# Two tiles' gate columns per branch-B unit, projected one unit later in a streaming encoder layer

## The chip, the cores and the metric

The kernel runs on one core of one Trainium2 chip. The metric is the device time of one execution in microseconds. The kernel before takes 2224.91 us, the median of three runs (2220.69 to 2227.12). The engines go by their names in the profile: PE is TensorE, DVE is VectorE, ACT is ScalarE, POOL is GpSimd, SP is SyncE (here it only issues DMAs).

## The reference

One layer over a prompt of 2048 rows and over 8 running sequences of 16 rows (one more tile of 128 rows), width 1024. Two mixers work side by side on the same normed input `h`: branch A, a differential softmax attention with 4 heads of two 64-wide parts, and branch B, a stick-breaking attention with 8 heads of 64.

```python
h, gate = adaln_modulate(x, c, norm_g, w_ada, b_ada)
qa, ka, va, za, qb, kb, vb, zb, ga, gb = split(h @ w_in)   # 4 x 512, 4 x 512, 2 x 1024 columns
# branch A: p = softmax of two score sets, w = p1 - lam * p2, oa = w @ va
# branch B: z = qb @ kb.T / 8
log_1m = where(kpos < qpos, log_sigmoid(-z), 0)
log_a  = log_sigmoid(z) + reverse_cumsum(log_1m) - log_1m
ob     = where(kpos < qpos, exp(log_a), 0) @ vb
ya = (rms_norm(oa) * silu(za)) @ w_branch_a
yb = (ob * silu(zb)) @ w_branch_b
y  = (sigmoid(ga) * ya + sigmoid(gb) * yb) @ w_out
x  = x + gate * y
```

The 2048 columns `ga` and `gb` of `h @ w_in` are the gate columns that this change moves. Nothing needs them before the last stage, which merges the branches.

## The kernel before, in words

**Units and tiles.** The projections and the prompt's attention are cut into 8 units, `u` = 0 to 7. Unit `u` is one pair of heads, `h = u // 2`, of branch A (`kind` 0, even `u`) or branch B (`kind` 1, odd `u`). In each unit 17 tiles of 128 rows are worked: first the sample rows (`t = NT = 16`), then the prompt's tiles 0 to 15. So there are 136 steps `(u, t)`.

**Projection.** For a step, `project` multiplies the tile's `h`, kept as two f16 halves, with the unit's 512 columns of `w_in`, also two halves: 24 matmuls of 128x512 at L467 into a bank `ps_mm`, in 12 pieces of two. ACT, DVE and, in branch A, POOL then make queries, keys and values of them. `h` of a tile comes from DRAM (`fetch_h`, 512 KB) into one of three buffers `hs`, taken in turn; a load into a buffer must wait for the last matmul that reads what lies there.

**Gates.** A unit of branch B also owns 512 gate columns: `GATES[u]` has width 512 for odd and 0 for even `u`. So a step of branch B has 24 more matmuls at L543 (`gate_piece`) into the one bank `ps_t`, an ACT evacuation at L548 into the one buffer `gt`, and a store of 256 KB at L551 into `g_d[t]`. The same bank `ps_t` serves the transposes of queries and keys (L561, L565) and small column sums (L235). A step of branch A has no gates. Only the last five tiles of unit 7 (`late`) have theirs put off to the end, with pieces of their own.

**Scores.** `scores` works one tile of queries against all keys up to it, in chunks of 512 keys: two matmuls (L708, L709) into one of three banks `ps_s`, and a masking one (L712) on the diagonal. There are `2 * (t // 4 + 1)` chunks for tile `t`, so 80 in a unit. In branch B each chunk gets two sigmoids on ACT (L134), a running product on DVE (L682), a multiplication on POOL (L688), then the f16 halves on ACT (L616) and DVE (L619), a transposing DMA (L626, `wt<-sc_n`), and the product with the values on PE (L769, L770). In branch A there is a maximum on DVE (L602), the exponentials on ACT, the same transposing DMA, and L765 to L767 on PE. Tiles with high `t` are long, those with low `t` short.

**What sets the order.** The projections' pieces stand in one `line`; the loop at the end takes as many of them per scoring step as an estimate of that step's length says (`position`, `take`), about five steps ahead of the scores (`LEAD`). So while unit 1's last tiles are scored, unit 2's first tiles are projected. The pieces of scoring, projecting and preparing weights are interleaved by cost. The framework's scheduler then orders each engine's instructions and may move one behind others where its operands come later.

**Weight buffers.** 16 buffers of 4 KB per partition (`wa`, `wb`) go round in the list `free`. A unit's cut weights take four (`bufs[0:4]`), its gate weights four more (`bufs[4:8]`); `begin` gives them back when the next unit's first step starts. `prepare_unit` takes buffers for the unit after, and so do the key and norm passes (`norms`).

Of the kernel before, what the change touches and what calls it, by code (L numbers as in the profile page):

```python
# [21 lines left out]
AF = mybir.ActivationFunctionType  # L22
# [6 lines left out]
KT = D // P  # L29
# [4 lines left out]
NT = SEQ // P  # L34
# [28 lines left out]
LATE_ORDER = (NT - 3, NT - 1, NT - 2, NT - 5, NT - 4)  # L63
LATE_SHARE = (0, 20, 20, 20)
LEAD = 5.0
TILE_TIME = 0.6
SAMPLE_TIME = 0.3

GATES = [(u // 2 * 512, u % 2 * 512) for u in range(8)]
# [55 lines left out]
def layer_kernel(ctx: ExitStack, tc: tile.TileContext, a: dict):  # L125
    nc = tc.nc
    V, S, G, T = nc.vector, nc.scalar, nc.gpsimd, nc.tensor
    load = nc.sync.dma_start
# [11 lines left out]
    def kept(x):  # L140
        tc.keep_in_program_order(x)
        return x
# [45 lines left out]
    g_d = [dram.tile([P, 2 * D], F32, name=f"g_d{t}") for t in range(NT + 1)]  # L188
# [14 lines left out]
    free = buffers_of_4k("wa", 8)  # L203
# [7 lines left out]
    def bank(tag, dt=F32):  # L211
        return ps.tile([P, 512 if dt == F32 else 1024], dt, tag=tag, name=f"ps_{tag}", bufs=BANKS[tag])
# [120 lines left out]
    units = [None] * 8  # L333
# [68 lines left out]
    def finish_unit(u):  # L402

        U = units[u]
        sw, sh = U["sw"], sh_box[0]
        sc = con.tile([P, 7], F32, name=f"usc{u}")

        V.tensor_tensor(out=sc[:, 0:1], in0=U["fsq"], in1=nh2, op=ALU.mult)
        sq = scales(sc[:, 0:1], con, f"sq{u}")

        V.tensor_tensor(out=sc[:, 1:2], in0=sw[:, 1:2], in1=sh[:, 1:2], op=ALU.mult)
        V.tensor_tensor(out=sc[:, 2:3], in0=sc[:, 1:2], in1=sq[:, 0:1], op=ALU.mult)

        V.tensor_scalar(out=sc[:, 3:4], in0=sq[:, 1:2], scalar1=sq[:, 1:2], scalar2=0.125, op0=ALU.mult, op1=ALU.mult)
        V.tensor_scalar(out=sc[:, 4:5], in0=sc[:, 3:4], scalar1=-1.0, scalar2=None, op0=ALU.mult)

        if U["kind"] == 0:
            V.tensor_tensor(out=sc[:, 5:6], in0=sq[:, 1:2], in1=ls[:, 1:2], op=ALU.mult)
        else:
            V.tensor_scalar(out=sc[:, 5:6], in0=sq[:, 1:2], scalar1=2.0 ** -STICK, scalar2=None, op0=ALU.mult)  # L420
        if "sg" in U:

            V.tensor_tensor(out=sc[:, 6:7], in0=U["sg"][:, 1:2], in1=sh[:, 1:2], op=ALU.mult)
        U["sc"], U["sq"], U["k"], U["v"] = sc, sq, {}, {}
# [13 lines left out]
    def late(u, t):  # L438
        return u == 7 and NT - LATE <= t < NT

    def fetch_h(u, t):
        ahead[u, t] = hs[len(fetched) % 3].bitcast(F16).rearrange("p (f k n) -> p f k n", f=2, n=P)
        fetched.append(t)
        load(out=ahead[u, t], in_=hT_d[t // 4][:, t % 4, :, :, :])

    def project(U, t):

        kind, h, sc, sq = U["kind"], U["h"], U["sc"], U["sq"]
        g, i = t // 4, t % 4
        box = {}  # L450
# [18 lines left out]
        def piece(n):  # L469
            if n == 0:  # L470
                start()
            for j in range(2 * n, 2 * n + 2):
                mm(j)
            if n == 11:
                finish()
# [54 lines left out]
                load(out=s_d[U["u"]][:, 6:8, :], in_=vt.rearrange("p c f d -> p c (f d)"))  # L530
            U["q16", t], U["k16", t] = qb, k16

        g0, gw = GATES[U["u"]]
        per = 1024 // gw if gw else 0

        def gate_piece(n):

            if n == 0:
                box["g"] = bank("t")
            for j in range(per * n, per * n + per):  # L540
                hi, wi = ((0, 0), (0, 1), (1, 0))[j % 3]
                k = j // 3
                x = T.matmul(box["g"][:, 0:gw], box["h"][:, hi, k, :], U["wg"][k // per][:, k % per, wi, :], start=(j == 0), stop=(j == 3 * KT - 1))  # L543
                if late(U["u"], t) and j == per * n:
                    kept(x)
            if per * n + per == 3 * KT:
                gt = gts[:, 0:512]
                x = S.activation(out=gt[:, 0:gw], in_=box["g"][:, 0:gw], func=AF.Identity, scale=sc[:, 6:7])  # L548
                if late(U["u"], t):
                    kept(x)  # L550
                load(out=g_d[t][:, g0 : g0 + gw], in_=gt[:, 0:gw])  # L551

        U["gates", t] = box, [lambda n=n: gate_piece(n) for n in range(3 * KT // per if gw else 0)]
        return [lambda n=n: piece(n) for n in range(12)] + ([] if late(U["u"], t) else U.pop(("gates", t))[1])

    def transpose_qk(U, t):
        g, i = t // 4, t % 4
# [424 lines left out]
    def begin(u, t):  # L982
        if t == NT:
            if u > 0:
                free.extend(units[u - 1]["bufs"])
            finish_unit(u)

    def projection(m):
        u, t = steps[m]
        made = []  # L990

        def piece(i):
            if i == 0:
                begin(u, t)
                made.extend(project(units[u], t))
            if i == H_AT and not at_hand and m + 1 < len(steps) and steps[m + 1] not in ahead:
                fetch_h(*steps[m + 1])
            made[i]()

        return [lambda i=i: piece(i) for i in range(12 + (0 if late(u, t) else 3 * GATES[u][1] // 128))]  # L1000

    def late_gates(t):

# [418 lines left out]
    for n in range(len(steps) + 2):  # L1422
        made, qk, side = [], [], []
        if n < len(steps):
            u, t = steps[n]
# [215 lines left out]
```

## Time and profile before

| | |
|---|---|
| median of three runs | 2224.91 us (2220.69 to 2227.12) |
| the profiled execution, its own time | 2226.87 us |
| its span, first to last instruction | 2225.0 us |
| PE busy | 2048.1 us, 92% of the span |
| DVE / ACT / POOL busy | 1743.2 / 1605.3 / 719.5 us |
| mean granted PE clock | 0.98 |
| projection matmuls, L467 | 3120, busy 391.7 + 380.1 us |
| gate matmuls, L543 | 1632 (68 tiles of 24), busy 243.6 + 151.3 us |

Times are microseconds from the start of the span unless marked ns. A matmul's mean ns is its own length from start to end; matmuls overlap, so 24 in a row take much less than 24 of these. In the groups of instructions, what stands after the second bar is the idle time of the engine just before them, and what ended it. Windows cut the span into stretches and give each engine's busy time in them, the granted PE clock (PEclk) and the share of the DMA engines.

### The profile page before, as it was taken

What the parts mean: (1) busy time and instruction counts of PE and PEld (TensorE: products, weight loads), DVE (VectorE), ACT (ScalarE), POOL (GpSimd) and SP (SyncE); (2) the same over time, 40 slices, a digit from 0 to 9 for tenths busy, and PEclk for the clock granted to TensorE, in tenths of its full rate; (3) what the DMA queues carried; (4) which work ended last, traced back from release to release, by engine and by line L of the source; (5) the groups of instructions that cost most, each with busy time, mean ns of one, the idle gap of its engine ahead of it and who ended that gap; (6) DMA issues with size and microseconds to landing.
All of it is one profiled execution on the core that took longest, in us unless ns stands there. A gap on an engine that the chain in (4) does not pass through costs nothing.

```text
span 2225.0 us, 41210 instructions
## 1 busy us (share of the span) xinstructions
PE 2048.1 (92%) x14472; PEld 1089.3 (49%) x14472; DVE 1743.2 (78%) x3787; ACT 1605.3 (72%) x3212; POOL 719.5 (32%) x620
## 2 busy tenths in 40 slices
PE   3999999999999999999989998999997789899997
PEld 1545555555555455555554544555454344444443
DVE  5668868889886788988678888887689778787864
ACT  3978677788877787978777788876588575666531
POOL 0523024366311444742034365301345312211210
PEclk9999999999999999999999999999999899999999
DMA  9777669799796889979888999876677999889752
GB/s 333 261 246 183 128 151 224 181 221 209 184 266 164 217 199 207 212 192 227 190 207 203 182 237 223 231 171 136 151 165 174 192 280 251 217 250 235 188 155 67
DMA packets 824977, 451.03 MB, mean 203 GB/s; under 512 B 556122, under 2 KB 763274, under 8 KB 824256
## 3 DMA queue, kind: packets, MB, share of 16 engines
q1 hardware_dynamic: 823820, 448.01, 82.6%
q8 instruction: 113, 1.85, 0.4%
q14 instruction: 96, 0.79, 0.1%
q10 hardware_dynamic: 948, 0.39, 0.1%
HBM read 229.87 MB, written 86.02 MB: 142 GB/s over the span
## 4 chain that ended last, share of the span: by engine, by line
PE 27%; DVE 8%; DMA 7%; ACT 5%; issue 3%; POOL 2%; SPq 1%; DVEq 0%; POOLq 0%; ACTq 0%
PE ps_mm L467 7%; PE ps_t L543 6%; PE ps_o L1540 5%; PE ps_mm L1506 3%; DMA wt<-sc_n 2%; PE ps_s L708 1%; DVE sc_n L682 1%; PE ps_s L709 1%; DMA hs<-hT_d 1%; DMA hs<-o_d 1%; DMA dwt<-dsc 1%; ACT sc_p L134 1%; POOL sc_p L688 1%; PE ps_o L769 1%; ACT ps_s L134 1%
## 5 line engine op out<-in xcount | busy, mean ns | idle before, releaser
L688 POOL TENSOR_TENSOR sc_p<-sc_p,sc_n 128x127 f32<-128x127 f32 (+7 forms) x192 | 312.2, 1629 | 665.5 <-DVE sc_n L682 516.0
L467 PEld LDWEIGHTS <-hs 128*128 128x128 f16 x3120 | 293.3, 99 | 326.3 <-DMA hs<-hT_d 11.6
L467 PE MATMUL ps_mm<-wa,hs 128*128 128x512 f16 x1590 | 391.7, 382 | 10.8 <-DMA hs<-hT_d 9.2
L467 PE MATMUL ps_mm<-wb,hs 128*128 128x512 f16 x1530 | 380.1, 382 | 0.0
L682 DVE TENSOR_TENSOR_SCAN sc_n<-ps_s,sc_n,zero_t 128x512 f32<-128x512 f32 x192 | 245.4, 1278 | 30.6 <-ACT ps_s L134 25.1
L543 PE MATMUL ps_t<-wa,hs 128*128 128x512 f16 x1020 | 243.6, 381 | 3.3 <-DVE qst L576 2.3
L543 PEld LDWEIGHTS <-hs 128*128 128x128 f16 x1632 | 154.9, 98 | 186.2 <-DVE qst L576 6.3
L708 PE MATMUL ps_s<-k,qst 128*128 128x512 f16 (+3 forms) x640 | 222.8, 349 | 24.1 <-DVE sc_n L682 20.7
L619 DVE TENSOR_TENSOR sc_n<-sc_p,sc_n 128x128 f16<-128x128 f32 (+7 forms) x192 | 213.6, 1115 | 37.3 <-ACT sc_n L616 36.7
L134 ACT ACTIVATE sc_p<-ps_s,usc 128x512 f32<-128x512 f32 (+3 forms) x320 | 204.7, 640 | 36.0 <-PE ps_s L709 24.3
L709 PE MATMUL ps_s<-k,qst 128*128 128x512 f16 (+3 forms) x640 | 223.1, 349 | 0.0
L616 ACT CAST sc_n<-sc_p 128x128 f16<-128x128 f32 (+7 forms) x192 | 155.6, 811 | 60.6 <-POOL sc_p L688 59.9
L134 ACT ACTIVATE ps_s<-ps_s,usc 128x512 f32<-128x512 f32 (+3 forms) x320 | 197.0, 616 | 0.0
L543 PE MATMUL ps_t<-wb,hs 128*128 128x512 f16 x612 | 151.3, 382 | 7.8 <-DMA hs<-hT_d 4.4
L769 PE MATMUL ps_o<-v,wt 128*128 128x128 f16 x1088 | 134.4, 223 | 25.5 <-DMA wt<-sc_n 25.5
L1540 PE MATMUL ps_o<-wo,wb 128*128 128x512 f16 x624 | 144.8, 388 | 1.7 <-ACT wb L1314 1.7
L602 DVE TENSOR_SCALAR_CACHE_REDUCE sc_p<-ps_s,usc 128x512 f32<-128x512 f32 (+3 forms) x160 | 106.2, 664 | 33.3 <-PE ps_s L709 22.0
L1549 POOL TENSOR_TENSOR x<-m,x 128x512 f32<-128x512 f32 x32 | 47.0, 1468 | 255.4 <-DVE m L1544 161.8
L769 PEld LDWEIGHTS <-wt 128*128 128x128 f16 x1088 | 100.4, 100 | 54.3 <-DMA wt<-sc_n 29.6
L770 PE MATMUL ps_o<-v,wt 128*128 128x64 f16 x1088 | 126.2, 195 | 0.0
L682 DVE TENSOR_TENSOR_SCAN sc_n<-ps_s,zero_t 128x128 f32<-128x128 f32 (+3 forms) x128 | 104.1, 814 | 26.2 <-ACT ps_s L134 26.2
L1506 PEld LDWEIGHTS <-wa 128*128 128x128 f16 x816 | 77.8, 98 | 92.7 <-issue 6.3
(380 smaller groups left out, 4538.5 us busy)
## 6 DMA issues: line engine op xcount, KB each, us to landing
hs<-hT_d SPq DMA_DIRECT2D x132, 512.0 KB, 4.7
g_d<-gt SPq DMA_DIRECT2D x68, 256.0 KB, 4.7
out_dram<-pr SPq DMA_DIRECT2D x204, 64.0 KB, 3.3
o_d<-o SPq DMA_DIRECT2D x136, 64.0 KB, 2.3
wa<-g_d SPq DMA_DIRECT2D x17, 512.0 KB, 4.2
wb<-g_d SPq DMA_DIRECT2D x17, 512.0 KB
hs<-o_d SPq DMA_DIRECT2D x17, 512.0 KB, 4.0
wide<-in_w_ada_dram SPq DMA_DIRECT2D x8, 1024.0 KB, 12.6
```

The costliest lines, as they stand in the source:

```text
L134: i = S.activation(**kw)
L467: T.matmul(box["p"], box["h"][:, hi, k, :], U["w"][k][:, wi, :], start=(n == 0), stop=(n == 3 * KT - 1))
L543: x = T.matmul(box["g"][:, 0:gw], box["h"][:, hi, k, :], U["wg"][k // per][:, k % per, wi, :], start=(j == 0), stop=(j == 3 * KT - 1))
L616: x = S.copy(out=hi, in_=src)
L619: V.tensor_tensor(out=lo, in0=src, in1=hi, op=ALU.subtract)
L682: V.tensor_tensor_scan(out=dst[:, lo : lo + n][:, ::-1], data0=src[:, 0:n][:, ::-1], data1=zero_t[:, 0:1].to_broadcast([P, n]), initial=fi ...
L688: G.tensor_tensor(out=p[:, 0:m], in0=p[:, 0:m], in1=n[:, 1 : m + 1], op=ALU.mult)
L708: T.matmul(p[:, 0:n], qst[:, c, :], kk[:, c, 0:n], start=True, stop=False)
L709: T.matmul(p[:, 0:n], qst[:, 2 + c, :], kk[:, c, 0:n], start=False, stop=not diag)
L769: T.matmul(po[:, c * P : (c + 1) * P], wt[:, wj, :], vt[:, c, :, :], start=first, stop=False)
L1506: T.matmul(pb, st["u"][:, ui * 8 + br * 4 + k, :], wb[br * 4 + k // 2 * 2 + j][:, wi, k % 2, :], start=(n == 0), stop=(n == 11))
L1540: T.matmul(po, st["y"][:, yi * 8 + k, :], wo[j * 4 + k // 2][:, wi, k % 2, :], start=(n == 0), stop=(n == 3 * KT - 1))
```

## The change

A new table `LATER = 1, 3` names two tiles. In the units 1, 3 and 5 the gate matmuls of the tiles 1 and 3 are left out of branch B's step, and put into the step of the same tile in the next unit, 2, 4 or 6 of branch A, behind that step's own 24 matmuls. They use the earlier unit's gate weights (`units[u - 1]`) and scale, and the `h` that branch A's step has loaded anyway. So these steps of branch A have 24 pieces, and those of branch B 12. Six tiles with 144 matmuls, six evacuations and six stores are moved in all; no instruction is added or removed. Unit 7's gates stay where they were. The gate weights' four buffers are given back five steps later: `begin` frees the first four at the next unit's first step, as before, and the other four when its tile 4 is begun.

```diff
+LATER = 1, 3
...
+    def gated(u, t):
+
+        if t in LATER and u < 7:
+            return u - 1 if u % 2 == 0 and u > 0 else None
+        return u if u % 2 == 1 and not late(u, t) else None
...
-        U["gates", t] = box, [lambda n=n: gate_piece(n) for n in range(3 * KT // per if gw else 0)]
-        return [lambda n=n: piece(n) for n in range(12)] + ([] if late(U["u"], t) else U.pop(("gates", t))[1])
+        made = [lambda n=n: piece(n) for n in range(12)]
+        if late(U["u"], t):
+            U["gates", t] = box, gate_pieces(U)
+        elif gated(U["u"], t) is not None:
+            made += gate_pieces(units[gated(U["u"], t)])
+        return made
...
         if t == NT:
             if u > 0:
-                free.extend(units[u - 1]["bufs"])
+                free.extend(units[u - 1]["bufs"][0:4])
             finish_unit(u)
+        if u > 0 and u % 2 == 0 and t == max(x for x in LATER if x < NT) + 1:
+            free.extend(units[u - 1]["bufs"][4:])
...
-        return [lambda i=i: piece(i) for i in range(12 + (0 if late(u, t) else 3 * GATES[u][1] // 128))]
+        return [lambda i=i: piece(i) for i in range(12 if gated(u, t) is None else 24)]
```

`gate_pieces(W)` is the old body of `gate_piece` with the unit `W` that owns the gate columns in place of `U`. Lines of the changed kernel have other numbers: L474 there is L467 before, L552 is L543, L576 and L580 are L561 and L565, L723, L724 and L727 are L708, L709 and L712, L784 and L785 are L769 and L770.

The first place is PE's order where branch A's tile 2 of unit 2 has just been projected: the first score chunk of tile 15, the last and longest of unit 1 (`ps_s<-k,qst`). Before, between products with the values and the transposes of the next tile:

```order
L769 LDWEIGHTS wt
L769 MATMUL ps_o<-v,wt 128x128
L708 LDWEIGHTS qst
L708 MATMUL ps_s<-k,qst 128x512
L709 LDWEIGHTS qst
L709 MATMUL ps_s<-k,qst 128x512
L712 LDWEIGHTS idb
L712 MATMUL ps_s<-masks,idb 128x128
L561 LDWEIGHTS k_6211
L561 MATMUL ps_t<-id_192,k_6211 128x128
```

Now, at the same score chunk, with `hs_180` the `h` of tile 1:

```order
L474 MATMUL ps_mm<-wa_172,hs_182 128x512
L784 LDWEIGHTS wt
L784 MATMUL ps_o<-v,wt 128x128
L723 LDWEIGHTS qst
L723 MATMUL ps_s<-k,qst 128x512
L724 LDWEIGHTS qst
L724 MATMUL ps_s<-k,qst 128x512
L727 LDWEIGHTS idb
L727 MATMUL ps_s<-masks,idb 128x128
L785 LDWEIGHTS wt
L785 MATMUL ps_o<-v,wt 128x64
L552 LDWEIGHTS hs_180
```

All 24 gate matmuls of tile 1 follow there in one piece; the scheduler has put them behind tile 2's columns and six matmuls of tile 3's (`hs_182`), not straight behind tile 1's.

The second place is PE's order where unit 2's own scores begin (tile 0, chunks of 128 keys). Before, this chunk stood among products with unit 1's values, and 14 matmuls into tile 5's projection:

```order
L467 LDWEIGHTS hs_181
L467 MATMUL ps_mm<-wb_1428,hs_181 128x512
L769 LDWEIGHTS wt
L769 MATMUL ps_o<-v,wt 128x128
L770 LDWEIGHTS wt
L770 MATMUL ps_o<-v,wt 128x64
```

Now the last gate matmuls of tile 3 (`hs_182`) stand ahead of it, and the projection is 19 matmuls into tile 4:

```order
L552 LDWEIGHTS hs_182
L552 MATMUL ps_t<-wa_173,hs_182 128x512
L723 LDWEIGHTS qst
L723 MATMUL ps_s<-k,qst 128x128
L724 LDWEIGHTS qst
L724 MATMUL ps_s<-k,qst 128x128
L727 LDWEIGHTS idb
L727 MATMUL ps_s<-masks,idb 128x64
L723 LDWEIGHTS qst
L723 MATMUL ps_s<-k,qst 128x128
```

So at this point 48 gate matmuls more, and 19 of the projection fewer, have been done since tile 14 of unit 1 than before.

The third place is PE's order where branch B gives the gates up, at a diagonal chunk of unit 2's tile 14 (384 keys), while unit 3's tile 2 is projected. Before, tile 1's gates stood ahead of it:

```order
L543 LDWEIGHTS hs_182
L543 MATMUL ps_t<-wb_1424,hs_182 128x512
L708 LDWEIGHTS qst
L708 MATMUL ps_s<-k,qst 128x384
L709 LDWEIGHTS qst
L709 MATMUL ps_s<-k,qst 128x384
L712 LDWEIGHTS idb
L712 MATMUL ps_s<-masks,idb 128x64
L467 LDWEIGHTS hs_180
L467 MATMUL ps_mm<-wa_170,hs_180 128x512
```

Now the transposes of a finished tile stand ahead of it:

```order
L580 LDWEIGHTS qbuf_214
L580 MATMUL ps_t<-id_192,qbuf_214 128x128
L723 LDWEIGHTS qst
L723 MATMUL ps_s<-k,qst 128x384
L724 LDWEIGHTS qst
L724 MATMUL ps_s<-k,qst 128x384
L727 LDWEIGHTS idb
L727 MATMUL ps_s<-masks,idb 128x64
L474 LDWEIGHTS hs_180
L474 MATMUL ps_mm<-wa_175,hs_180 128x512
```

By unit 3's first scores 48 gate matmuls are gone from the row.

More of the change, by code (lines that the diff above doesn't have):

```diff
@@ L531, in finish @@
             U["q16", t], U["k16", t] = qb, k16
[L533 to L551, printed above, removed]
@@ L553, in project, with gate_pieces, gate_piece @@
-        U["gates", t] = box, [lambda n=n: gate_piece(n) for n in range(3 * KT // per if gw else 0)]
-        return [lambda n=n: piece(n) for n in range(12)] + ([] if late(U["u"], t) else U.pop(("gates", t))[1])
+        def gate_pieces(W):
+            g0, gw = GATES[W["u"]]
+            per = 1024 // gw
+            def gate_piece(n):
+                if n == 0:
+                    box["g"] = bank("t")
+                for j in range(per * n, per * n + per):
+                    hi, wi = ((0, 0), (0, 1), (1, 0))[j % 3]
+                    k = j // 3
+                    x = T.matmul(box["g"][:, 0:gw], box["h"][:, hi, k, :], W["wg"][k // per][:, k % per, wi, :], start=(j == 0), stop=(j == 3 * KT - 1))
+                    if late(W["u"], t) and j == per * n:
+                        kept(x)
+                if per * n + per == 3 * KT:
+                    gt = gts[:, 0:512]
+                    x = S.activation(out=gt[:, 0:gw], in_=box["g"][:, 0:gw], func=AF.Identity, scale=W["sc"][:, 6:7])
+                    if late(W["u"], t):
+                        kept(x)
+                    load(out=g_d[t][:, g0 : g0 + gw], in_=gt[:, 0:gw])
+            return [lambda n=n: gate_piece(n) for n in range(3 * KT // per)]
```

## The prediction, made before the changed kernel ran

> **What bounds the kernel now.** I read the page's busy times first, then the chain that ended last, then the waits stage by stage.
>
> ```profile
> PE 2048.1 (92%) x14472; PEld 1089.3 (49%) x14472; DVE 1743.2 (78%) x3787; ACT 1605.3 (72%) x3212; POOL 719.5 (32%) x620
> PE 27%; DVE 8%; DMA 7%; ACT 5%; issue 3%; POOL 2%; SPq 1%; DVEq 0%; POOLq 0%; ACTq 0%
> PE ps_mm L467 7%; PE ps_t L543 6%; PE ps_o L1540 5%; PE ps_mm L1506 3%; DMA wt<-sc_n 2%; PE ps_s L708 1%; DVE sc_n L682 1%; PE ps_s L709 1%; DMA hs<-hT_d 1%; DMA hs<-o_d 1%; DMA dwt<-dsc 1%; ACT sc_p L134 1%; POOL sc_p L688 1%; PE ps_o L769 1%; ACT ps_s L134 1%
> ```
>
> PE leads with 92%, and the gate matmuls (L543) hold 6% of the span on the chain, second only to the projection. The change takes no matmul away; it can win only idle time of PE. So the question is where PE idles, and whether the moved matmuls land there. To cut the span by stages I count score matmuls in their order:
>
> ```profile
> L708 PE MATMUL ps_s<-k,qst 128*128 128x512 f16 (+3 forms) x640 | 222.8, 349 | 24.1 <-DVE sc_n L682 20.7
> ```
>
> 640 are 80 in each unit, 2 x (t // 4 + 1) for tile t, so the first of each tile is known. The windows below run from one such start to another. First three: from tile 12 of units 0, 2 and 4 (branch A) to the first scores of units 1, 3 and 5; there the B tiles 1 and 3 are projected now. Then three for each A unit 2, 4, 6: from tile 14 of the B unit before to the A unit's tile 0, from there to tile 4, and to tile 9.
>
> ```profile
> core 0: us, PE busy (x) PEld busy (x) DVE busy (x) ACT busy (x) POOL busy (x), PEclk, DMA share, GB/s
> 222.00:294.00 72.00, 69.13 (x486) 37.79 (x486) 52.75 (x136) 46.17 (x95) 0.00 (x0) 1.00 0.61 127
> 629.00:699.00 70.00, 67.50 (x469) 37.01 (x468) 49.60 (x135) 48.86 (x103) 2.24 (x2) 1.00 0.85 204
> 1041.00:1111.00 70.00, 69.37 (x470) 37.77 (x468) 49.27 (x133) 47.99 (x101) 2.24 (x2) 0.98 0.88 205
> 482.00:524.00 42.00, 38.48 (x310) 21.40 (x310) 40.55 (x49) 40.89 (x81) 31.82 (x24) 1.00 0.98 207
> 524.00:554.00 30.00, 27.24 (x222) 15.63 (x220) 28.01 (x70) 23.10 (x55) 18.12 (x19) 0.94 0.91 206
> 554.00:594.00 40.00, 40.00 (x280) 21.99 (x277) 34.03 (x104) 34.74 (x81) 14.39 (x16) 1.00 0.70 192
> 891.00:932.00 41.00, 37.44 (x299) 20.64 (x298) 40.04 (x47) 40.01 (x77) 31.56 (x23) 1.00 1.00 207
> 932.00:964.00 32.00, 27.26 (x230) 15.93 (x228) 25.48 (x69) 23.23 (x56) 18.96 (x19) 0.95 0.92 194
> 1305.00:1349.00 44.00, 38.01 (x298) 20.64 (x298) 40.31 (x49) 40.30 (x78) 30.86 (x23) 1.00 0.99 221
> 1349.00:1382.00 33.00, 28.59 (x225) 16.15 (x224) 26.49 (x73) 25.82 (x60) 18.71 (x19) 0.90 0.96 195
> ```
>
> The reader is to see two regimes. In the first three rows PE is busy 96 to 99% and DVE and ACT 64 to 75%: PE bounds them. In B's tail (482:524 and its like) DVE and ACT are at 92 to 98% and PE idles 3.5, 3.6 and 6.0 us. In the next stretch it idles 2.8, 4.7 and 4.4 us; after that, in 554:594, not at all. These waits are, in three of the stretches:
>
> ```profile
> L708 PE MATMUL ps_s<-k,qst 128*128 128x512 f16 (+2 forms) x18 | 6.4, 355 | 4.6 <-DVE sc_n L682 4.6
> ...
> L769 PE MATMUL ps_o<-v,wt 128*128 128x128 f16 x43 | 5.3, 228 | 2.8 <-DMA wt<-sc_n 2.8
> ...
> L467 PE MATMUL ps_mm<-wa,hs 128*128 128x512 f16 x28 | 7.0, 379 | 1.3 <-DMA hs<-hT_d 1.3
> ```
>
> In B's tail PE waits for DVE's running product to free a score bank (482:524). Then it waits for the last transposed weights (524:554). In 891:932 it waits 1.3 us for a load of `h` too.
>
> **The change part by part.** The price of a gate tile, from the chain in order of time:
>
> ```profile
> 1092.53 5.18 PE ps_t L543 x24
> ```
>
> 24 matmuls take 5.18 us in a row, 0.216 each. Three units with two tiles each are 6 x 5.18 = 31.1 us, taken out of one place and put into another.
>
> *What goes.* 10.4 us of PE work from each of the first three windows. Bounds: all of it, as PE is 96 to 99% busy there; or a third, if the softmax chains behind it set the pace. What speaks for less than all is that the gates cover waits of branch A's tail, which stand at
>
> ```profile
> L765 PE MATMUL ps_o<-v,wt 128*128 128x128 f16 x60 | 10.7, 219 | 1.3 <-ACT o L744 1.0 <-DMA wt<-sc_n 0.2
> L765 PE MATMUL ps_o<-v,wt 128*128 128x128 f16 x54 | 9.5, 219 | 2.5 <-DMA wt<-sc_n 2.5
> L765 PE MATMUL ps_o<-v,wt 128*128 128x128 f16 x56 | 10.5, 226 | 0.6 <-DMA wt<-sc_n 0.6
> ```
>
> for the three windows. With the cover gone each may grow by about its own size, 1.5 us in the mean; I take 85%, 8.8 us each, **-26.4 us**. What is late next there is the same PE row: 60 us of work are left against 50 on DVE.
>
> *What comes.* By the order of instructions, 29 matmuls more stand between unit 1's tile 14 and unit 2's tile 0 (48 gates more, 19 of the projection fewer), which is 6.3 us; the other 19, 4.1 us, follow until tile 9. For units 3 and 5 before 4 and 6 the counts are the same; in unit 6 the projection even runs 17 ahead by tile 9 and gives that back in unit 7. The first stretch has 3.5, 3.6 and 6.0 us of PE's idle time, and its waits fall where gate matmuls now stand: they need only weights and an `h` that are long there. I count three quarters of the 13.1 us as filled, 9.8, since a block of 24 cannot fall into every wait. In the second stretch PE waits at the last 16 products with unit 1's weights. Between the last score chunk of its tile 15 and them stood 66 projection matmuls, and now 69 and four of a gate: seven more, 1.5 us of the wait in each unit, 4.5 us. The third stretch has no idle time, so it pays in full. Bounds of the filling: nothing, as DVE and ACT are the bound in the tail and score chunks now stand behind gates; or all, 6.3 + 8.3 + 10.4 = 25.0 us. I take 9.8 + 4.5 = 14.3, by the rows of these two stretches: 31.1 - 14.3 = **+16.8 us**.
>
> *What moves with them.* Each gate tile has an ACT evacuation and a store on SP's queue:
>
> ```profile
> L548 ACT ACTIVATE gt<-ps_t,usc x68: 664/687/720, 233.0 to 1747.2; 128x512 f32<-128x512 f32 x68
> hs<-hT_d SPq DMA_DIRECT2D x132, 512.0 KB, 4.7
> g_d<-gt SPq DMA_DIRECT2D x68, 256.0 KB, 4.7
> ```
>
> Two evacuations are 1.4 us more on an ACT at 40.9 of 42 us. But 19 projection matmuls, four fifths of a tile, go out of that stretch, and a tile's columns cost ACT an evacuation (L481) of
>
> ```profile
> L481 ACT ACTIVATE pr<-ps_mm,usc 128x512 f32<-128x512 f32 x5 | 3.7, 748 | 0.0
> ```
>
> and the halves of `v`, `k` and queries besides. I take the sum as zero; either way it is under 1 us each. The `h` of tile 1 is held longer, so the load for tile 4 into its buffer waits on SP for the last gate matmul; tile 5's now stands ahead of it. From that matmul to tile 4's first, 18 projection matmuls (3.9 us), five score chunks of two passes (2.2 us) and some 60 small products and transposes stand in PE's order, over 6 us against 4.7 to land. I take nothing; if it is late, it costs 1 to 2 us, as the 1.3 above. What stands behind it on SP are a gate store and transposes of B's last tiles, which have not been made yet at that time. Holding four of 16 weight buffers five steps longer costs nothing: the list had them free then.
>
> **Sum:** -26.4 + 16.8 = -9.6 us on the profiled execution's 2226.87 us, 2217.3. That execution stands 2.0 us above the median of 2224.91, so on the median **2215 us**.
>
> One more price stands in the trace. After the 2.76 us gap PE runs slower:
>
> ```profile
> 542.92 0.23 PE L769 MATMUL ps_o<-v,wt 128*128 128x128 f16 x1 [2.76 <-DMA wt<-sc_n]
> 543.94 3.66 PE L467 MATMUL ps_mm<-wb,hs 128*128 128x512 f16 x10
> 547.93 2.75 PE L467 MATMUL ps_mm<-wa,hs 128*128 128x512 f16 x12
> ```
>
> Ten matmuls take 3.66 us, then twelve 2.75; the windows show a clock of 0.94, 0.95 and 0.90, so 1.8, 1.6 and 3.3 us of clock lost in the three second stretches, 6.7 in all. A gap of 3 us thus costs about 2 more. Since 1.5 us of the gap at most goes, I keep the loss as it is.
>
> The Trainium skill, "TensorE: Matmul & The Clock Gate", Part 1 (the HAM clock gate), has the clock halved after an idle window of about 3.4 us; the trace shows it after 2.76. By that rule the change could also hurt: a wait at L765 that outgrew the window would lose about 1.7 us each (half of the window, an estimate from that page), and the sum would be -4.5 instead of -9.6.
>
> **The rivals.**
> *All gaps are filled.* The gates push unit 1's last products late enough that their weights have landed, the second gap goes, and with it the slow stretch. For it: only 2.8 to 4.7 us are missing. Against: only seven matmuls more stand ahead. It gives -26.4 + 31.1 - 25.0 = -20.3, and -27.0 without the slow stretches, so 2198 to 2205, 2201 us.
> *Cost for cost.* The tail is DVE's and ACT's. A block of 24 matmuls, 5.2 us, between two score chunks leaves three banks of 1.28 us of product each,
>
> ```profile
> L682 DVE TENSOR_TENSOR_SCAN sc_n<-ps_s,sc_n,zero_t 128x512 f32<-128x512 f32 x14 | 17.9, 1276 | 0.6
> ```
>
> 3.8 us, to feed them. Then they starve 1.4 us a block, and PE's filling is lost again: -26.4 + 26 to 31, so 2225 us. Against: as long blocks stand there now (19 projection matmuls and twelve products).
> *Slower: branch B's windows don't shrink.* If the softmax chains of the tiles 12 to 15 (exponentials, sums, halves, a transposing DMA) set the pace once the gates are gone, PE only idles more at L765. For it: those waits exist. Against: 96 to 99% busy, DVE and ACT with 17 to 26 us to spare. With a third saved it is -10.4 + 16.8 = +6.4, 2231 us, and 2 us more for each gap that slows the clock, 2231 to 2237. It decides for slower from the point where less than 16.8 of 31.1 us is saved.
> That the change doesn't do what it says is out: the order shows the gates gone and come.
>
> **How the numbers follow.** The forecast has 0.50 (its own range 2208 to 2222), all gaps filled 0.13, cost for cost 0.22, slower 0.15. A measurement tells about 0.3%, 6.7 us, from no change, so faster is below 2218.2. The forecast lies there with three parts of four, 0.38; with 0.13 of the second case that is 0.51. The same: 0.12 of the forecast and 0.20 of cost for cost, 0.32. Slower: 0.15 and 0.02, 0.17. The range 2202 to 2230 leaves out about half of the all-filled case and most of the slower one, 0.19 in all.
>
> **What would show it.** Right: the windows from tile 12 to unit 1, 3 and 5's first scores are 61 to 63 us instead of 70 to 72; from tile 14 to tile 9 in units 2, 4 and 6 they are 4 to 7 us longer; L708's wait for DVE in B's tail falls from 4 to 5 us to under 2, L769's for the DMA falls by 1 to 2. Wrong: L765's waits in the first windows grow by more than 5 us each; or B's tail grows by more than 5 us with DVE below 90%; or waits for `hs<-hT_d` at tile 4.

## The result, and the profile after

The changed kernel takes 2253.7 us, the median of four runs (2252.93 to 2256.36), against 2223.26 us for the kernel before beside it (four runs, 2220.69 to 2227.12). The ratio is 1.0143, with a 95% interval of 1.0122 to 1.0163: **30 us slower**. The forecast was 2215 us, with a range of 2202 to 2230. Four runs beside the experiments below (one of e7, two of e10, one of the kernel before) took 3358 us or more, and the ratios leave them out. The profiled execution took 2256.36 us, its span is 2254.5 us.

The page of the changed kernel, busy times and the chain that ended last by engine and by line:

```profile
PE 2063.2 (92%) x14472; PEld 1090.7 (48%) x14472; DVE 1755.1 (78%) x3787; ACT 1600.5 (71%) x3212; POOL 721.1 (32%) x620
...
PE 25%; DVE 6%; DMA 5%; ACT 3%; issue 3%; POOL 2%; SPq 0%; DVEq 0%; POOLq 0%; ACTq 0%
PE ps_o L1557 6%; PE ps_mm L1523 5%; PE ps_t L552 5%; PE ps_mm L474 4%; DVE sc_n L697 2%; DMA hs<-hT_d 1%; DMA hs<-o_d 1%; PE ps_s L723 1%; PE ps_s L724 1%; DMA wt<-sc_n 1%; DMA dwt<-dsc 1%; PE ps_s L1330 1%; PE ps_t L898 1%; DMA o_d<-o 1%; POOL sc_p L703 1%
```

The same 14472 matmuls take 15.1 us more of busy time, 2063.2 against 2048.1, and PE's share is 92% as before. The page alone would hardly show a loss. The stages do. Windows of the changed kernel, cut at the same score matmuls as in the prediction: for the units 1, 3 and 5 from tile 12 of the unit before to the first scores, and from there to the unit's tile 4; for unit 2 the three stretches from unit 1's tile 14 to its own tile 9; and unit 7 in three stretches (from tile 12 of unit 6 to the first scores, to tile 4, to tile 14).

```profile
core 0: us, PE busy (x) PEld busy (x) DVE busy (x) ACT busy (x) POOL busy (x), PEclk, DMA share, GB/s
222.30:284.80 62.50, 59.13 (x438) 33.06 (x438) 51.84 (x133) 40.89 (x87) 0.00 (x0) 1.00 0.67 131
284.80:323.90 39.10, 33.83 (x211) 17.71 (x210) 23.95 (x52) 29.40 (x69) 8.52 (x10) 0.91 0.59 128
484.90:532.80 47.90, 45.36 (x325) 24.45 (x325) 37.73 (x48) 39.10 (x76) 29.95 (x23) 0.96 0.95 188
532.80:559.40 26.60, 26.60 (x225) 15.38 (x224) 22.48 (x64) 23.75 (x55) 14.38 (x15) 1.00 0.99 219
559.40:606.70 47.30, 44.66 (x314) 24.19 (x311) 42.13 (x115) 38.66 (x91) 18.72 (x20) 1.00 0.65 178
641.90:704.50 62.60, 60.73 (x435) 33.54 (x435) 49.88 (x135) 44.28 (x98) 2.24 (x2) 0.97 0.83 203
704.50:742.00 37.50, 32.50 (x210) 17.38 (x209) 26.20 (x61) 31.20 (x73) 9.97 (x12) 0.91 0.80 201
1059.40:1122.70 63.30, 60.71 (x435) 33.45 (x435) 50.22 (x135) 44.30 (x97) 2.24 (x2) 0.97 0.88 203
1122.70:1161.00 38.30, 33.23 (x209) 17.70 (x208) 26.20 (x61) 31.21 (x73) 9.94 (x12) 0.91 0.76 201
1485.30:1543.80 58.50, 58.50 (x434) 33.09 (x432) 47.44 (x124) 39.73 (x85) 0.00 (x0) 1.00 0.66 157
1543.80:1597.40 53.60, 44.45 (x298) 23.97 (x297) 37.48 (x81) 29.57 (x68) 14.89 (x14) 0.94 0.57 139
1597.40:1739.20 141.80, 126.12 (x908) 67.91 (x907) 119.66 (x167) 105.92 (x214) 61.85 (x41) 0.94 0.68 147
```

Windows of the kernel before, those of these stretches that the prediction did not show (first scores to tile 4 of the units 1, 3 and 5, and unit 7):

```profile
294.20:322.10 27.90, 27.63 (x186) 15.16 (x185) 19.58 (x43) 23.64 (x58) 6.62 (x8) 1.00 0.56 151
698.70:728.20 29.50, 28.30 (x192) 15.80 (x191) 22.80 (x48) 22.29 (x54) 8.32 (x10) 1.00 0.74 200
1111.50:1141.00 29.50, 28.30 (x191) 15.80 (x190) 22.80 (x48) 22.40 (x55) 9.49 (x10) 1.00 0.82 200
...
1461.50:1529.80 68.30, 67.35 (x465) 36.63 (x464) 50.64 (x134) 47.45 (x98) 0.00 (x0) 1.00 0.63 141
1529.80:1573.80 44.00, 37.70 (x228) 19.37 (x227) 31.65 (x60) 23.96 (x57) 14.94 (x13) 0.92 0.63 144
1573.80:1707.00 133.20, 125.12 (x954) 69.38 (x953) 113.89 (x183) 106.74 (x218) 55.58 (x42) 0.96 0.75 160
```

The reader is to see that the windows on which the forecast rested did shrink, from 70 to 72 us to 62.5 to 63.3. But right behind them the stretch to tile 4 grew from 27.9, 29.5 and 29.5 us to 39.1, 37.5 and 38.3. PE is idle there for 5 us each (39.1 less 33.83 and its like) where it was idle for 0.3 to 1.2, and its granted clock is 0.91 where it was 1.00.

What happens there, in the order of time. PE of the changed kernel at unit 1's first scores (start, length, instruction, and in brackets the idle time before it and its releaser):

```profile
291.65 0.28 PE L576 MATMUL ps_t<-id,k 128*128 128x128 f16 x2 [0.96 <-DVE k L324]
...
295.15 0.29 PE L580 MATMUL ps_t<-id,qbuf 128*128 128x128 f16 x2 [2.24 <-ACT qbuf L508]
297.46 0.40 PE L580 MATMUL ps_t<-id,qbuf 128*128 128x128 f16 x2 [2.03 <-DVE qbuf L509]
297.65 5.59 PE L474 MATMUL ps_mm<-wb,hs 128*128 128x512 f16 x13
```

ACT of the changed kernel at that time:

```profile
283.30 1.16 ACT L135 ACTIVATE sc_p<-sc_p,nm 128x1024 f32<-128x1024 f32 x1
...
286.70 1.14 ACT L135 ACTIVATE sc_n<-sc_n,nm 128x1024 f32<-128x1024 f32 x1
...
287.95 1.28 ACT L135 ACT_TABLE_LOAD   x1
...
290.50 0.35 ACT L319 ACTIVATE k<-ps_mm,usc 128x128 f16<-128x128 f32 x1
...
294.57 0.53 ACT L508 ACTIVATE qbuf<-ps_mm,usc 128x256 f16<-128x256 f32 x1
```

And the kernel before at its first scores, ACT, then PE:

```profile
287.88 0.37 ACT L318 ACTIVATE k<-ps_mm,usc 128x128 f16<-128x128 f32 x1 [1.20 <-DVE v L323]
288.14 1.14 ACT L134 ACTIVATE sc_p<-sc_p,nm 128x1024 f32<-128x1024 f32 x1
...
292.79 1.28 ACT L134 ACT_TABLE_LOAD   x1
...
295.33 0.46 ACT L501 ACTIVATE qbuf<-ps_mm,usc 128x256 f16<-128x256 f32 x1
```

```profile
289.64 4.70 PE L543 MATMUL ps_t<-wa,hs 128*128 128x512 f16 x21
```

Branch A's last tiles end with wide exponentials on ACT; then ACT loads the table of branch B's sigmoids. It works without a pause there. Before, the next tile's keys are converted ahead of the exponentials (287.88 us) and its queries soon behind the table load (295.33), and tile 3's gate matmuls stand on PE during just these microseconds. In the changed kernel no gate matmul stands there, the keys come behind the table load (290.50), and the queries behind the first sigmoids too (294.57). PE comes to the transposes of these keys and queries (L576, L580) before ACT, and DVE behind it, have converted them. PE waits 0.96, 2.24 and 2.03 us; then 13 matmuls take 5.59 us, 0.43 each, twice the 0.216 of the prediction.

The groups of instructions over the whole span show which waits came and which went. The changed kernel:

```profile
L723 PE MATMUL ps_s<-k,qst 128*128 128x512 f16 (+3 forms) x640 | 222.3, 349 | 36.0 <-DVE sc_n L697 28.6 <-DVE sc_p L617 4.3 <-DVE sc_n L617 1.8
...
L784 PE MATMUL ps_o<-v,wt 128*128 128x128 f16 x1088 | 130.4, 223 | 14.7 <-DMA wt<-sc_n 14.7
...
L580 PE MATMUL ps_t<-id,qbuf 128*128 128x128 f16 x544 | 55.9, 222 | 12.3 <-ACT qbuf L508 6.7 <-DVE qbuf L509 5.6
...
L576 PE MATMUL ps_t<-id,k 128*128 128x128 f16 x272 | 38.1, 221 | 11.4 <-DVE k L324 5.0 <-ACT gt L557 4.9 <-ACT qst L591 1.5
```

The kernel before:

```profile
L769 PE MATMUL ps_o<-v,wt 128*128 128x128 f16 x1088 | 134.4, 223 | 25.5 <-DMA wt<-sc_n 25.5
...
L565 PE MATMUL ps_t<-id,qbuf 128*128 128x128 f16 x544 | 55.0, 220 | 0.0
...
L561 PE MATMUL ps_t<-id,k 128*128 128x128 f16 x272 | 37.9, 219 | 4.7 <-DVE fsq L371 2.2 <-DVE k L323 1.4 <-ACT gt L548 1.1
```

The transposes wait 19.0 us more (12.3 and 11.4 against 0.0 and 4.7), and the scores 11.9 more (36.0 against 24.1). The products with transposed weights wait 10.8 us less: the filling in branch A.

The whole span, cut into stages. "Work" is the columns of all matmuls that start in the stage, at the measured 5.18 us for 24 matmuls of 512 columns. "PE idle" is the stage's length less PE's busy time in it. "Clock" is the time at a lower granted clock, times what was missing to 1. Differences of the profiled executions, after less before, in us:

| stage | wall | work | PE idle | clock |
|---|---|---|---|---|
| tile 12 to first scores, units 1, 3, 5 | -24.2 | -29.3 | +1.8 | +1.7 |
| first scores to tile 4, units 1, 3, 5 | +28.0 | +6.9 | +12.7 | +10.2 |
| tile 4 to tile 14, units 1, 3, 5 | -4.3 | -6.9 | +2.0 | 0.0 |
| branch A: tile 14 to tile 12 of units 2, 4, 6 | +24.1 | +33.1 | -9.1 | -1.7 |
| unit 7, to its tile 14 | +8.5 | -3.7 | +9.5 | +3.4 |
| start and end of the kernel | -2.4 | 0.0 | -2.4 | -1.6 |

Idle time at a lower clock is counted in both of the last columns. What else is left of a row, 2 us at most, isn't explained.

### The profile page after: what moved, and what is told of

It reads as the page before. It is cut to its first block, busy times and chain, and to the rows that moved or that the text cites. A ratio compares the mean times of both kernels' runs of the same rounds, so it can differ in the third digit from the quotient of the medians.

```text
span 2254.5 us, 41236 instructions
## 1 busy us (share of the span) xinstructions
PE 2063.2 (92%) x14472; PEld 1090.7 (48%) x14472; DVE 1755.1 (78%) x3787; ACT 1600.5 (71%) x3212; POOL 721.1 (32%) x620
## 5 line engine op out<-in xcount | busy, mean ns | idle before, releaser
L703 POOL TENSOR_TENSOR sc_p<-sc_p,sc_n 128x127 f32<-128x127 f32 (+7 forms) x192 | 318.9, 1664 | 593.8 <-DVE sc_n L697 554.1
L474 PEld LDWEIGHTS <-hs 128*128 128x128 f16 x3120 | 294.9, 99 | 329.0 <-issue 19.4
L474 PE MATMUL ps_mm<-wb,hs 128*128 128x512 f16 x1530 | 386.3, 386 | 9.6 <-DVE sc_n L697 6.2
L474 PE MATMUL ps_mm<-wa,hs 128*128 128x512 f16 x1590 | 390.6, 382 | 1.6 <-DMA wb<-in_w_in_dram 1.6
L634 DVE TENSOR_TENSOR sc_n<-sc_p,sc_n 128x128 f16<-128x128 f32 (+7 forms) x192 | 226.6, 1183 | 39.4 <-ACT sc_n L631 38.6
L723 PE MATMUL ps_s<-k,qst 128*128 128x512 f16 (+3 forms) x640 | 222.3, 349 | 36.0 <-DVE sc_n L697 28.6
L552 PEld LDWEIGHTS <-hs 128*128 128x128 f16 x1632 | 156.3, 99 | 198.1 <-DVE qst L591 10.5
L552 PE MATMUL ps_t<-wa,hs 128*128 128x512 f16 x918 | 219.8, 381 | 6.6 <-DVE qst L591 3.7
L724 PE MATMUL ps_s<-k,qst 128*128 128x512 f16 (+3 forms) x640 | 222.6, 350 | 0.0
L552 PE MATMUL ps_t<-wb,hs 128*128 128x512 f16 x714 | 177.1, 389 | 8.2 <-DVE qst L591 3.7
L784 PE MATMUL ps_o<-v,wt 128*128 128x128 f16 x1088 | 130.4, 223 | 14.7 <-DMA wt<-sc_n 14.7
L785 PE MATMUL ps_o<-v,wt 128*128 128x64 f16 x1088 | 123.5, 196 | 0.0
L617 DVE TENSOR_SCALAR_CACHE_REDUCE sc_n<-ps_s,usc 128x512 f32<-128x512 f32 (+3 forms) x160 | 106.2, 664 | 20.0 <-PE ps_s L724 17.6
L515 POOL TENSOR_TENSOR rot<-pr,rope 128x256 f32<-128x256 f32 x68 | 63.0, 926 | 180.8 <-ACT pr L488 113.9
```

The lines of the kernel that those rows point to most:

```text
L474: T.matmul(box["p"], box["h"][:, hi, k, :], U["w"][k][:, wi, :], start=(n == 0), stop=(n == 3 * KT - 1))
L552: x = T.matmul(box["g"][:, 0:gw], box["h"][:, hi, k, :], W["wg"][k // per][:, k % per, wi, :], start=(j == 0), stop=(j == 3 * KT - 1))
L617: V.tensor_scalar(out=dst[:, lo : lo + n], in0=p[:, 0:n], scalar1=sc_pos, scalar2=None, op0=ALU.mult, op1=ALU.max, accum_out=job["mx"][:, ...
L634: V.tensor_tensor(out=lo, in0=src, in1=hi, op=ALU.subtract)
L703: G.tensor_tensor(out=p[:, 0:m], in0=p[:, 0:m], in1=n[:, 1 : m + 1], op=ALU.mult)
L723: T.matmul(p[:, 0:n], qst[:, c, :], kk[:, c, 0:n], start=True, stop=False)
```

## The experiments

The first theory is **cover**: PE's 96 to 99% in branch B was no bound, and the gate matmuls covered waits for ACT, DVE and the transposing DMA. Against it stood that the loss is made elsewhere: by the addition in branch A, by the buffers held longer, or by the order alone, since the planner spreads pieces by their number (**pace**). All diffs are against the changed kernel; each kernel ran beside the kernel before, and the ratio is to that.

**e1_removed: the gates leave branch B, and come nowhere.** 23 of 24 matmuls of each moved tile are left out, 29.8 us of PE's work.

```diff
-        if t in LATER and u < 7:
-            return u - 1 if u % 2 == 0 and u > 0 else None
...
+                    if t in LATER and W["u"] < 7 and j > 0:
+                        continue
...
```

> Of the six moved gate tiles one matmul of 24 is left in branch B, and nothing is put into branch A (these gate columns are then partial sums); evacuations and stores stay. 138 matmuls, 29.8 us of PE work, are gone. Theory 'cover': in the kernel before, the gates of tiles 1 and 3 stood in front of transposes that wait for ACT while ACT works off the last exponentials of branch A (about 7 us with a table load); without them PE idles about 5 us at the first scores of units 1, 3 and 5 and its clock is halved for a while (about 3.4 us), so little of 29.8 us shows: 2210 to 2225 us. Rival 'price is in branch A': PE bounds branch B, the removal shows nearly whole, 2195 to 2200 us.

Measured: 2217.62 us, 0.9979 (0.9966 to 0.9992), in cover's range. Of 29.8 us of PE's work, 3.5 us show in the medians (2221.09 before). The windows before the first scores shrink by 22.2 us, and the first stretch behind them grows by 13.3. But the gap that cover expected at the transposes isn't there (waits of 0.2 us at most in each unit); of the 13.3 us 4.9 are work from the neighbouring stages, 4.8 idle time and 2.5 clock.

**e2_both: the gates stay in branch B, and are made in branch A once more.**

```diff
-        if t in LATER and u < 7:
-            return u - 1 if u % 2 == 0 and u > 0 else None
+        if t in LATER and u % 2 == 0 and u > 0:
+            return u - 1
```

> The six gate tiles are projected twice: in branch B as before, and again in branch A as in the change. 144 matmuls, 31.1 us of PE work, are added. Theory 'cover': branch A pays most of it, except for the wait at the last transposed weights that it fills (10 to 15 us in all): 2238 to 2248 us, with no new gap at the first scores of units 1, 3 and 5. Rival 'price is in branch A': the whole loss of the change plus what the removal saved, 2250 to 2260 us.

Measured: 2254.1 us, 1.0151 (1.0134 to 1.0168), 33 us more. That is the rival's range, and above cover's: the addition costs more than cover had it. Branch A pays 24.2 us for it, as in the changed kernel (24.1), and unit 7 pays 14.5. Taking the gates away from branch B, as the changed kernel does beyond this, gives next to nothing. The removal alone (3.5 us won) and the addition alone (33.0 us lost) make 29.5 us together, and the change lost 30.

**e3_tile1, e4_tile3 and v2_tile2: one tile alone**, tile 1, tile 3 and, later, tile 2.

```diff
-LATER = 1, 3
+LATER = (1,)
```

> Only tile 1's gates are moved, tile 3's stay in branch B. Theory 'cover': tile 3's gates, which stand just ahead of the first scores of units 1, 3 and 5, still cover ACT's exponentials, so the new gap there is small (under 2 us); branch A pays the 5.2 us in the unfilled tail of branch B: 2220 to 2232 us. Rival 'any gate is as good as another': half of the change's loss, 2238 us.

> Only tile 3's gates are moved, tile 1's stay in branch B. Theory 'cover': the gap at the first scores of units 1, 3 and 5 opens (4 to 5 us idle and a halved clock), and branch A's gap at the last transposed weights is filled: the first costs 2 to 4 us a unit beyond what is saved, the second gives 4 to 6 back against 5.2 paid: 2225 to 2238 us. Rival 'any gate is as good as another': half of the change's loss, 2238 us.

> Tile 2's gates alone are moved, as far as possible from both bad places: tile 3's and 4's stay as cover at the first scores of units 1, 3 and 5. Theory 'cover': the removal still shows only in part, the addition in branch A costs its 5.2 us less what fills the wait at the last transposed weights: 2218 to 2232 us. Rival 'each moved tile costs the same': 2238 to 2244 us.

Measured: 2237.26 us, 1.0073 (1.0058 to 1.0088), for tile 1; 2243.63, 1.0099 (1.0082 to 1.0116), for tile 3; 2234.1, 1.0053 (1.0032 to 1.0074), for tile 2. Each is slower alone, and each lies above cover's range; tile 1 has the rival's 2238 us. With tile 3 moved the gap at the first scores opens as in the changed kernel (idle 12.8 us more, clock 10.2, in three units); with tile 1 or 2 it doesn't. So tile 3's step decides there, by its missing matmuls or by its 12 pieces instead of 24; these three runs don't tell which. The parts don't add up, 16 and 22 us (by the ratios) against 32.

**e5_hold: no gate is moved, but the gate weights' buffers are freed five steps later.**

```diff
-        if t in LATER and u < 7:
-            return u - 1 if u % 2 == 0 and u > 0 else None
```

> No gate is moved; only the four gate buffers of units 1, 3 and 5 are given back five steps later, as in the change. If the other rotation of the weight buffers were the cause of the loss: 2240 to 2255 us. Every other theory: no change, 2217 to 2227 us.

Measured: 2224.12 us, 0.9999 (0.9985 to 1.0013). The buffers cost nothing. This run also gives the scatter: against the kernel before, branch B's units agree within 0.1 us, branch A's within 2.3.

**e6_refill: the change, and tile 3's gates in branch B once more**, 72 matmuls and 15.5 us of work on top of the changed kernel.

```diff
-        if t in LATER and u < 7:
+        if t in LATER and u < 7 and (u % 2 == 0 or t == 1):
```

> The change as it is, but tile 3's gates are also projected in branch B again, as before, so that they are projected twice. 72 matmuls, 15.6 us of PE work, are added to the change. Theory 'cover': they run while PE would wait for ACT at the first scores of units 1, 3 and 5 and keep its clock up, so they cost nothing or little: 2246 to 2258 us against the change's 2254, with the gap there under 1.5 us idle. Rival 'PE's work counts': 2265 to 2270 us.

Measured: 2248.44 us, 1.0108 (1.0083 to 1.0133). With 15.5 us more of work it isn't slower than the changed kernel (1.0122 to 1.0163), and rather faster, though the intervals overlap. At the first scores idle and clock loss are back to within 1.7 us of before. That is as cover had it; but tile 3's step has its 24 pieces again too, so this run can't tell the matmuls from the count of pieces.

**e7_paced and e8_paced_both: branch B's step keeps its 24 pieces, twelve of them empty.** e7 moves tile 3 alone, e8 both tiles. The instructions are those of e4 and of the changed kernel; only the planner's count differs.

```diff
         elif gated(U["u"], t) is not None:
             made += gate_pieces(units[gated(U["u"], t)])
+        elif U["u"] % 2 == 1:
+            made += [lambda: None] * 12
...
-        return [lambda i=i: piece(i) for i in range(12 if gated(u, t) is None else 24)]
+        return [lambda i=i: piece(i) for i in range(12 if gated(u, t) is None and (u % 2 == 0 or late(u, t)) else 24)]
```

> Tile 3's gates alone are moved, and branch B's step of tile 3 keeps 24 pieces, twelve of them empty, so that the interleaving of projection and scores in branch B is paced as before; by PE's order two blocks of gates now stand otherwise around unit 1's first scores. If the loss with tile 3 moved (2243.6 us) came of the changed pace: 2220 to 2230 us. Theory 'cover': the 24 matmuls are missing at that place all the same: 2236 to 2246 us.

> The whole change, and branch B's steps of tiles 1 and 3 keep 24 pieces, twelve of them empty. With tile 3 alone this took the loss from 22 to 5 us. If the pace of the interleaving in branch B is what turns the saving there into waits: 2230 to 2240 us, with branch B's stages shorter than before by 8 to 15 us in all. If the missing cover is what does it, and tile 3 alone was an accident of order: 2248 to 2256 us.

Measured: 2227.87 us, 1.0017 (1.0005 to 1.003), and 2229.37 us, 1.0055 (1.0032 to 1.0079). Tile 3's loss falls from 0.99% to 0.17%, the whole change's from 1.43% to 0.55%. Cover, as it was expected here (2236 to 2246 and 2248 to 2256 us), is refuted: the matmuls are missing, and most of the loss is gone. At unit 1's first scores e7 has on PE

```profile
296.38 0.29 PE L582 MATMUL ps_t<-id,qbuf 128*128 128x128 f16 x2 [0.86 <-ACT qbuf L508]
297.01 0.28 PE L582 MATMUL ps_t<-id,qbuf 128*128 128x128 f16 x2 [0.35 <-DVE qbuf L509]
```

and on ACT

```profile
288.41 0.37 ACT L319 ACTIVATE k<-ps_mm,usc 128x128 f16<-128x128 f32 x1 [1.20 <-DVE v L324]
...
293.32 1.28 ACT L135 ACT_TABLE_LOAD   x1
...
295.87 0.45 ACT L508 ACTIVATE qbuf<-ps_mm,usc 128x256 f16<-128x256 f32 x1
```

No gate matmul stands there either, from 280 us to 301.67. But the keys are converted ahead of the exponentials again and the queries soon behind the table load, as in the kernel before, and PE waits 1.2 us instead of 5.2. e8 has on PE

```profile
291.50 3.19 PE L552 MATMUL ps_t<-wa,hs 128*128 128x512 f16 x14
...
296.36 2.32 PE L552 MATMUL ps_t<-wa,hs 128*128 128x512 f16 x10
```

and on ACT

```profile
286.22 0.47 ACT L508 ACTIVATE qbuf<-ps_mm,usc 128x256 f16<-128x256 f32 x1 [0.56 <-DVE k L324]
286.59 1.14 ACT L135 ACTIVATE sc_p<-sc_p,nm 128x1024 f32<-128x1024 f32 x1
...
291.23 1.28 ACT L135 ACT_TABLE_LOAD   x1
```

Here the next tile's queries are converted ahead of the exponentials, and 24 gate matmuls (tile 4's, which stay in unit 1) stand from the table load on. In the changed kernel there is no gate matmul at that place. So pace is shown: the same work in another order costs 20 us less (0.88% of 2223), and the stretch from the first scores to tile 4 grows by 3.4 us instead of 28.0. What decides at this place is the order on ACT, as the units 1, 3 and 5 of all runs show. Where the keys are converted 2.5 us behind the start of the table load or more (the changed kernel, e4, and the units 1 and 3 of e9), the transposes around it wait 5.0 to 5.2 us a unit. Where they are converted ahead of it, in every other case, the transposes wait 1.2 us at most, in e7 with no gate matmul near.

**e9_units13: only the units 1 and 3 give their gates away.**

```diff
-        if t in LATER and u < 7:
+        if t in LATER and u < 5:
...
```

Unit 5's gate weights are given back as in the kernel before.

> The change for units 1 and 3 only; unit 5 keeps its gates and units 6 and 7 their pieces. In the change's trace the stages of units 1 to 4 lost about 18 us and the stages of units 5 to 7 about 14, 8.5 of them in unit 7's scores, where no gate was moved. If that last part comes of unit 6's order: 2238 to 2243 us with unit 7's stage as before (245 us). Rival: unit 7's stage is long for another reason, and it stays at 254 us: 2246 to 2250 us.

Measured: 2242.94 us, 1.0102 (1.0078 to 1.0126). Unit 7, which grew by 8.5 us in the changed kernel, grows by 1.6 here, so its loss comes from what is changed in the units 5 and 6. In e2, where of these two only unit 6 differs, it grows by 14.5: unit 6's addition is enough.

**e10_removed8: eight tiles, t = 1, 3 to 15, of the units 1, 3 and 5 lose 23 of 24 matmuls each**, and nothing is added; the edit is e1's with more tiles. That is 119.1 us of PE's work.

```diff
-LATER = 1, 3
+LATER = tuple(range(1, NT, 2))
```

> As e1_removed, with the eight odd tiles of units 1, 3 and 5 in place of two: 552 matmuls, 119 us of PE work, are gone from branch B, and nothing is added. Theory 'ACT and DVE stand close behind PE in branch B': PE's work there falls by 16% and the time by much less, 20 to 50 us (2172 to 2202). Rival 'only the order around two tiles was unlucky': 80 us or more (under 2142).

Measured: 2219.4 us, 0.9992 (0.9973 to 1.0011): no gain, and neither of the two ranges. From the first scores of unit 1 to its tile 9, and on to its tile 14, windows of e10:

```profile
285.40:393.10 107.70, 91.65 (x633) 50.20 (x632) 84.50 (x169) 81.96 (x184) 40.49 (x36) 0.95 0.76 180
393.10:484.40 91.30, 77.91 (x575) 41.46 (x574) 75.93 (x104) 72.54 (x143) 45.27 (x32) 0.96 0.99 224
```

and of the kernel before:

```profile
294.20:389.70 95.50, 92.00 (x648) 50.28 (x647) 79.22 (x158) 73.48 (x164) 36.94 (x35) 1.00 0.81 199
389.70:482.30 92.60, 90.86 (x632) 47.95 (x631) 75.95 (x107) 73.71 (x147) 40.14 (x28) 1.00 0.85 197
```

In the second stretch PE is busy 13 us less, and its length is 1.3 us less; DVE and ACT do the same 76 and 73 us. The first stretch even grows, by 12.2 us. Over the span PE's waits for transposed weights are, in the groups of e10:

```profile
L784 PE MATMUL ps_o<-v,wt 128*128 128x128 f16 x1088 | 137.1, 226 | 61.8 <-DMA wt<-sc_n 61.5
```

61.5 us against 25.5. PE is busy 1966.7 us of e10's span of 2218.7, so it idles 252.0 us instead of 176.9; and with a mean granted clock of 0.964 instead of 0.980 it loses 35 us more to the clock. These 75 and 35 us stand in the place of the work that is gone. So PE, 96 and 98% busy in these two stretches before, did not bound them by the amount of its work, but about a third of what was taken out came back as slower matmuls and waits at half clock. PE's largest wait now is for the end of the softmax chains, whose last link is the transposing DMA; which link of a chain is the slowest was not tried.

Differences of the wall time of stages against the kernel before, in us, beside what the prediction had:

| stage | predicted | change | e1 | e2 | e4 | e6 | e7 | e8 | e10 |
|---|---|---|---|---|---|---|---|---|---|
| tile 12 to first scores, units 1, 3, 5 | -26.4 | -24.2 | -22.2 | +4.1 | -12.7 | -4.1 | -10.9 | -21.7 | -23.4 |
| first scores to tile 4 | 0 | +28.0 | +13.3 | 0.0 | +29.4 | +3.2 | +9.2 | +3.4 | +16.2 |
| tile 4 to tile 14 | 0 | -4.3 | +5.7 | -2.3 | -4.3 | +3.5 | -1.8 | +0.4 | -8.1 |
| branch A, units 2, 4, 6 | +16.8 | +24.1 | -7.2 | +24.2 | +11.9 | +21.3 | +8.4 | +19.5 | +4.5 |
| unit 7, to its tile 14 | 0 | +8.5 | +2.2 | +14.5 | -0.6 | +7.6 | -1.9 | +9.3 | +6.7 |

(The start and the end of the kernel hold no part of any edit, and are 2 to 13 us shorter in these profiled executions than in that of the kernel before. So the stages are compared, not their sums, and a few us in one of them say little. Of e7's 9.2 us in the second row 6.5 are work from the neighbouring stages, and 1.6 idle time.)

## Why the prediction was wrong

**What goes: this step failed.** It put 8.8 us of each 10.4 down as saved, "PE is busy 96 to 99% and DVE and ACT 64 to 75%: PE bounds them". (By the rows it is 64 to 73%, with 19 to 26 us to spare and not 17.) The windows themselves shrank almost as said, by 24.2 us against 26.4. But 28.0 us came back in the next stretch, and the removal by itself (e1) was worth 3.5 us. In that stretch PE waits for the next tile's keys and queries, which ACT now converts behind branch A's exponentials and the table load. A busy share near 100% says that PE had something to do, not that its work sets the time: in e10 119.1 us of such work went, and the time stayed. The Trainium skill, "Perfetto Trace Analysis", section Identifying the Most-Contended Engine, calls the busy share of matmuls no good measure of how close a kernel is to roofline, and names MFU (the share of the peak rate of arithmetic) and the busy share of the weight loads in its place. In the first window of before the weight loads have 37.79 of 72 us, 52%; no run here shows what that share says of a bound.

**What comes: its terms were mis-sized.** The wall grew by 24.1 us to tile 12, and by 29.4 to tile 9, where the sum of +16.8 ended. Of the 14.3 us of filling, 9.8 were to come in B's tail. The idle time there fell from 12.7 to 8.6 us in the three units, and 5.1 us of newly slow clock took that back (484.90:532.80: a clock of 0.96). The gap at the transposed weights went altogether (11.9 us of idle time and 6.8 of clock, tile 0 to tile 4 of the units 2, 4 and 6; 532.80:559.40 shows PE busy throughout), where 4.5 had been counted and the clock left as it was. In the third stretch, where there had been no idle time, 9.0 us came up (2.6 of 47.3 in 559.40:606.70), and 1.7 of clock. In all about 11 us were filled by tile 12, 9.1 of idle time and 1.7 of clock. That this is not far from 14.3 is luck, since it came in other places. The rest of what was missed is 2.0 us of work more than the gates themselves (33.1 against 31.1), which came in from the neighbouring stages, and 2 us that aren't explained.

**What moves with them: partly wrong.** Held buffers cost nothing, as said (e5). That unit 6's projection runs ahead was seen, and "gives that back in unit 7" was taken as free. It cost 8.5 us: 46 fewer matmuls (908 against 954) are on PE's row in unit 7's stretch from tile 4 to tile 14, and PE idles 15.7 us there (141.80 less 126.12) instead of 8.1. The number of pieces in a step, which the diff changes from 24 to 12, was not priced at all, as if it were nothing; by e8 it is worth 20 of the 30 us. That is the second step that failed.

**The rivals.** "Branch B's windows don't shrink" had 0.15. What it said of PE came true: it only idles more, and gaps slow the clock. But the windows did shrink; the wait fell behind them, at the transposes and not at L765, and the price of 2231 to 2237 was too low. "All gaps are filled" was right on the second gap, which went with its slow stretch, and wrong on the waits of the tail, which remain. "Cost for cost" (2225) is what e8 comes near, at 2229, in the number alone.

**What was to show it.** The windows of 61 to 63 us came (62.5, 62.6, 63.3). For tile 14 to tile 9, 4 to 7 us more were expected; 9.9 (121.8 against 111.9), 8.5 and 11.0 were measured. The wait of scores for DVE in unit 1's tail fell from 4.6 to 2.9 us and not under 2, and L769's wait for the DMA fell by more than was said. One of the signs of being wrong came too: B's tail grew by 6.5 us in the units 2 and 4, with DVE at 79% (37.73 of 47.9). The first windows alone looked right, and no sign looked at the stretch behind them.

What stays open: how the count of pieces puts ACT's exponentials ahead of the keys, and why the order with twelve pieces is worse beyond the first scores of branch B, the one place followed in detail; why e1, which keeps 24 pieces and has the gates out of branch B as e8 has, keeps less of the gain there (13.3 us given back at the first scores against 3.4); and why the losses of single tiles don't add up. No version that moves a gate and does the whole work beats the kernel before; e7 comes nearest, 0.17% slower.

## What to carry to other kernels

Before counting PE's work as saved, ask what PE would wait for in its place: lay ACT's and DVE's rows over the very microseconds that fall free, in the order that the changed program gives them, and follow the time past the next stage's start, where it may come back. Taking the work out altogether, or adding it twice, tests a bound in one run each: 119.1 us of "bound" work out changed the time by 0.1%, and 15.5 us put back in cost nothing. Where a planner spreads work by a count of pieces, a change of the count is a change of its own, and can be taken apart with empty pieces.

## What the runs showed of the hardware

In the places followed here the granted PE clock fell to a half around waits of 1 to 3 us. In the changed kernel, at unit 1's first scores, it is 0.5 from 296.12 us on for 6.83 us. That begins within the third of the waits of 0.96, 2.24 and 2.03 us, with only a few small matmuls between them:

```profile
296.00:300.00 4.00, 2.54 (x8) 1.11 (x9) 4.00 (x10) 4.00 (x10) 0.70 (x2) 0.52 0.14 33
```

By the measure of the table 3.4 us are lost there, 0.7 of them while PE still waits, beside 5.2 us of waiting. The kernel before had 2.76 us of waiting, then, from 543.24 us on, 3.41 us at half clock. One wait of 2.25 us in the changed kernel (to 328.15 us) has no such stretch behind it. The Trainium skill, "TensorE: Matmul & The Clock Gate", Part 1, has a free-running window of 3413 ns, and the clock halved after an idle window; the lengths agree (one and two windows), but none of these waits was that long by itself. Over the span, 12.0 of the 29.5 us that the profiled execution lost are clock.
